# Dense expert blocks loaded in pairs of 8 KB per partition, in a hybrid decoder step on one core

## The chip, the cores and the metric

The kernel runs on one core of one Trainium2 chip. The metric is the device time of one execution in microseconds (us), taken as the median over several runs. The profile shows one profiled execution; its engines are PE (TensorE matmul), PEld (TensorE weight load), DVE (VectorE), ACT (ScalarE), POOL (GpSimd) and SP (SyncE, which issues most transfers).

## The reference, cut to what matters

One layer of a hybrid decoder for 256 prompt tokens behind 16 meta tokens and 8 running sequences of 8 tokens each. A large input projection feeds a Conformer branch and a Mamba-2 branch, and an output projection joins them. Then comes the part that the change is about, a mixer over 16384 experts (128 x 128 product keys), of which each token uses 8 heads x 16:

```python
def peer_block(xb, w_q, keys, U, V):
    q = (xb @ w_q).reshape(T, PEER_HEADS, 2, D_KEY // 2)
    s = jnp.einsum('thcd,hckd->thck', q, keys).astype(jnp.float32)
    ...
    g = jax.nn.softmax(sc, axis=-1)
    act = jax.nn.gelu(jnp.einsum('thkd,td->thk', U[ids], xb), approximate=False)
    w = (g * act).astype(xb.dtype)
    return jnp.einsum('thk,thkd->td', w, V[ids])
```

U and V hold 16384 rows of 1024 floats, 64 MB each.

## The kernel before, in words

**Weights, to 628 us.** Each projection matrix comes in blocks of 128 outputs, 512 KB, 4 KB on each of the 128 partitions. `weight` (L241) lets SP load a block into a `wraw` tile (four buffers), ACT casts it to the high part `wh` (L217), POOL subtracts it to get the low part `wl` (L218; two buffers each), and PE multiplies with both parts.

**Experts, from 628 us.** The tokens are split. For 128 tokens (and a few of the rest, `x2e`) the used rows are gathered: 144 gathers (L1080, POOL issues, queue q0), each bringing for 128 partitions one row of U and one of V, 8 KB side by side in `wuv` (five buffers). Such a *pick* is a dot product on DVE (`pick_dot`, L1192), two small ACT instructions on `scg` (gelu, then the gate, L1194 and L1195), and a weighted sum on DVE (`pick_sum`, L1200).

For the other 176 tokens every expert is computed. `u_block` (L1261) takes 128 experts of U, one of 128 blocks of 512 KB: 8 accumulating f32 matmuls on PE (L1266, two instructions each on the chip), then ACT writes the gelu of the PSUM tile into `S` (L1268). PSUM has six tiles for this, so block b + 6 waits for `S(b)`. `v_block` (L1354) multiplies the blocks of V with S in a second pass (L1357). Between them, `g_step` builds the gates of a few tokens: DVE makes one-hot matrices `oh` (L1287, L1288, L1290), PE multiplies them to `pg` (24 small matmuls, L1295), and DVE multiplies `S` by it (L1302). 22 g steps for the first half of the experts lie among u blocks 66 to 127, 22 more at the start of the second pass.

Blocks are loaded by `block` (L1254) into a ring that reuses the weights' tiles: wraw, wh, wraw, wl in turn, eight tiles of 4 KB. SP issues the loads in order and waits for each tile to be free. Between the passes SP loads `nd<-x1d` (the residual, L1324), which PE adds into the accumulators `va` (L1326). After block 122 `finish` normalises the gathered tokens, with two `wraw` tiles for its output `out_y`.

**What sets the order.** Each engine runs its instructions in the order that the Tile scheduler wrote down: DVE's picks and g steps, and ACT's `scg` and `S`, stand in one fixed row each, and an instruction that waits holds all behind it on its engine. The scheduler's own estimates of when tiles come free decide how picks and blocks interleave. Gathers are also held to the pace of the dense blocks (`gather`, L1078).

Of the kernel before, what the change touches and what calls it, by code (L numbers as in the profile page):

```python
# [7 lines left out]
F32 = mybir.dt.float32  # L8
F32R = mybir.dt.float32r
# [7 lines left out]
D = 1024  # L17
KD = 8
# [34 lines left out]
CE = 1  # L53
LOW = 400
NW0 = 3
RB = 4
OH = 2
UV = 5
GLAG = 14
# [76 lines left out]
def body(tc, ia, oa, stop=None):  # L136
    nc = tc.nc
    with ExitStack() as top:
# [10 lines left out]
        def mm(*a_, **kw):  # L149
            i_ = nc.tensor.matmul(*a_, **kw)  # L150
            if pin[0]:
                tc.keep_in_program_order(i_)
# [18 lines left out]
        o_ = VEC["conf_w"][0]  # L171
# [20 lines left out]
        def act(out, in_, f, **kw):  # L192
            i_ = nc.scalar.activation(out, in_, f, **kw)  # L193
            chain(i_)
            return i_

        def pj(name="pj"):
            return ps.tile([128, PJ], F32, name=name, tag="pj", bufs=3)[:, :T]

        def pj2(name="pj"):  # L200
            return pj(name)[:, :T2]
# [14 lines left out]
        def split(h, l, src, on_pool=False, on_dve=False):  # L216
            (nc.vector.tensor_copy if on_dve else nc.scalar.copy)(h, src)  # L217
            (nc.gpsimd if on_pool else nc.vector).tensor_tensor(l, src, h.bitcast(F32), op=OP.subtract)  # L218
# [10 lines left out]
            nc.vector.tensor_copy(dst[2 * H:2 * H + n], r_)  # L229

        S0 = NQ * TS
        rb = [RB]

        def proj(out, w, act, first=True, last=True):
            for k in range(KD):
# [2 lines left out]
            for k in range(KD):  # L238
                mm(out, w[1][:, k, :], act(k)[0], start=False, stop=(last and k == KD - 1))

        def weight(src, i):  # L241
            raw = wp.tile([128, KD, 128], F32, name="wraw", bufs=rb[0])
            nc.sync.dma_start(raw, src[i].rearrange("p (k m) -> p k m", m=128))
            h = wp.tile([128, KD, 128], F32R, name="wh", bufs=2)
            l = wp.tile([128, KD, 128], F32R, name="wl", bufs=2)
            nw[0] += 1
            f_ = lm[0]
            on_dve = int((nw[0] + 1) * f_) > int(nw[0] * f_)
            split(h, l, raw, on_pool=not on_dve, on_dve=lm[0] == 1)
            return h, l  # L250
# [6 lines left out]
        def misc(shape, name):  # L257
            return ps.tile(shape, F32, name=name, tag="misc", bufs=2)

        wp = top.enter_context(tc.tile_pool(name="wp", bufs=1))  # L260
# [8 lines left out]
        dp = dt_scope.enter_context(tc.tile_pool(name="dp", bufs=1))  # L269
# [21 lines left out]

        raws, whs, wls = [], [], []
        for i in range(3):
            r_ = wp.tile([128, KD, 128], F32, name="wraw", bufs=rb[0])
            nc.sync.dma_start(r_, ia["w_in"][(4, 5, 0)[i]].rearrange("p (k m) -> p k m", m=128))
            raws.append(r_)
            for n_, l_ in (("wh", whs), ("wl", wls)):
                l_.append(wp.tile([128, KD, 128], F32R, name=n_, bufs=2) if i < 2 else
                          dp.tile([128, KD, 128], F32R, name=n_ + "3"))
            if i == 1:  # L300
                nc.sync.dma_start(hv, ia["hv"])
        nc.sync.dma_start(vec[:, o_:], ia["vec"][:, o_:])
# [17 lines left out]
        p = misc([128, T], "pn1")  # L320
# [4 lines left out]
        on, _ = VEC["n1"]  # L325
# [7 lines left out]
        t = tp.tile([128, T], F32, name="rst", tag="yo", bufs=2)  # L333
# [504 lines left out]
        for g in range(G):  # L838
            new = ssd(g, *tiles, sz)
            if g + 1 < G:  # L840
                tiles, steps = xbc(g + 1)
# [48 lines left out]
        for j in range(KD):  # L890
# [4 lines left out]
            p = pj2()  # L895
# [7 lines left out]
        for j in range(KD):  # L903
            w = weight(ia["w_o"], j)
            p = pj2()
# [13 lines left out]
        p = ps.tile([128, T], F32, name="pn2", tag="pb", bufs=1)  # L919
        nc.tensor.matmul(p[:, :T2], ones, csum[:, :T2], start=True, stop=False)  # L920
        nc.tensor.matmul(p[:, :T2], ones, sq[:, :T2], start=False, stop=True)
        o_ = VEC["conf_w"][0]
# [33 lines left out]
        for c_ in range(2):  # L956
            p = misc([128, 512], "px")
# [4 lines left out]
        p = misc([128, 4], "prs")  # L962
# [7 lines left out]
        if NX:  # L970
# [7 lines left out]
            for c_ in range(2):  # L978
                p = misc([128, 512], "px")
# [114 lines left out]
        for j in range(16):  # L1094
            w = weight(ia["w_q"], j)
            p = pj()
# [3 lines left out]
            p = misc([128, 3, NK], "psc")  # L1100
# [149 lines left out]
                self.tasks = []  # L1250

        nraw = [0]

        def block(src, i):  # L1254
            tag, nb = (("wraw", rb[0]), ("wh", 2), ("wraw", rb[0]), ("wl", 2))[nraw[0] % 4]
            nraw[0] += 1
            raw = wp.tile([128, D], F32, name="eraw", tag=tag, bufs=nb)
            nc.sync.dma_start(raw, src[i])
            return raw.rearrange("p (k m) -> p k m", k=KD)

        def u_block(b):  # L1261
            raw = block(ia["uT"], b)
            tag, nb = (("pj", 3), ("y", 2), ("pj", 3), ("y", 2), ("pj", 3), ("pb", 1))[b % 6]
            p = ps.tile([128, PJ], F32, name="pj", tag=tag, bufs=nb)[:, :T]
            for k in range(KD):
                i_ = nc.tensor.matmul(p[:, :ND], raw[:, k, :], nd[:, k, :], start=(k == 0), stop=(k == KD - 1))  # L1266
            ustep.append(i_.ins.name)
            nc.scalar.activation(Sv(b), p[:, :ND], AF.Gelu)  # L1268
# [61 lines left out]
        def finish(tiles, load):  # L1330
            n = len(tiles)
            rs = gp.tile([128, 4, n], F32, name="frs", bufs=2)
            o = [wp.tile([128, D], F32, name="wraw", bufs=rb[0]) for _ in tiles]
            for a, (src, t0, _) in enumerate(tiles):
                nc.scalar.activation(o[a][:, :512], src[0], AF.Square, accum_out=rs[:, 0, a:a + 1])
                nc.vector.tensor_copy(o[a][:, 512:], src[1])
                nc.vector.scalar_tensor_tensor(o[a][:, 512:], o[a][:, 512:], 1.0, src[1], op0=OP.mult, op1=OP.mult,
                                               accum_out=rs[:, 1, a:a + 1])
            nc.vector.tensor_tensor(rs[:, 2], rs[:, 0], rs[:, 1], op=OP.add)
            if load:  # L1340
                tc.keep_in_program_order(nc.scalar.preload_act_table_set("natural_log_exp_and_others"))
            rstd_of(rs[:, 3], rs[:, 2], D, gp, load=False)
            for a, (src, t0, L) in enumerate(tiles):
                r_, f_ = rs[:, 3, a:a + 1], fin[0]
                for c_ in range(2):
                    cs = slice(c_ * 512, c_ * 512 + 512)
                    if a == 0 and c_ == 0:
                        nc.scalar.activation(o[a][:, cs], src[c_], AF.Copy, scale=r_)
                        nc.gpsimd.tensor_tensor(o[a][:, cs], o[a][:, cs], f_[:, cs], op=OP.mult)
                    else:  # L1350
                        nc.vector.scalar_tensor_tensor(o[a][:, cs], src[c_], r_, f_[:, cs], op0=OP.mult, op1=OP.mult)
                    (nc.sync if c_ else nc.scalar).dma_start(oa["y"][t0:t0 + L, cs], o[a][:L, cs])
# [44 lines left out]
def layout(i):  # L1397
    f = {k: np.asarray(v) for k, v in i.items()}
# [23 lines left out]
    def put(name, a):  # L1422
# [29 lines left out]
        ccache=f["cache_conf"][0].reshape(NQ, 30, 8, 128).transpose(2, 3, 0, 1).reshape(8, 128, NQ * 30),  # L1452
        state=f["state_ssm"][0].reshape(NQ, G, 256, N).transpose(1, 3, 0, 2),
        peer_uv=np.concatenate([f["peer_u"][0], f["peer_v"][0]], 1),
        uT=f["peer_u"][0].reshape(128, 128, 8, 128).transpose(0, 3, 2, 1).reshape(128, 128, D),
        vE=f["peer_v"][0].reshape(128, 128, D),
        fnorm=f["final_norm_w"],
        n2row=f["norm2_w"][0],
        fn=feat(f["final_norm_w"]),
# [31 lines left out]
```

## Time and profile before

| | us |
|---|---|
| median of 3 runs (lowest, highest) | 1382.77 (1382.6, 1384.68) |
| the profiled execution | 1380.86 |
| its span in the profile | 1379.1 |
| PE busy in it | 1317.8 |
| DVE busy | 1013.5 |
| ACT busy | 529.0 |
| POOL busy | 567.5 |

The mean clock granted to TensorE was 0.982 of full speed. In the fences of the prediction, a row of the windows gives a stretch's start and end, its length, then for each engine its busy time with the number of instructions, then the granted clock, the mean busy share of the 16 DMA engines and the GB/s that they moved. A row of the waits gives the engine, what it was about to write and its line, then what ended the wait, the time in total, how often, and the longest. A queue's row has its packets, megabytes and the time of its packets as a share of 16 engines' span. A group's row has the operation with its shapes and count, busy time, mean ns of one, and the idle time before it with what ended it. A timeline's row has start, duration, engine, line, operation, and in brackets the idle time ahead with its releaser.

### The profile page before, as it was taken

What the parts mean: (1) busy time and instruction counts of PE and PEld (TensorE: products, weight loads), DVE (VectorE), ACT (ScalarE), POOL (GpSimd) and SP (SyncE); (2) the same over time, 40 slices, a digit from 0 to 9 for tenths busy, and PEclk for the clock granted to TensorE, in tenths of its full rate; (3) what the DMA queues carried; (4) which work ended last, traced back from release to release, by engine and by line L of the source; (5) the groups of instructions that cost most, each with busy time, mean ns of one, the idle gap of its engine ahead of it and who ended that gap; (6) DMA issues with size and microseconds to landing.
All of it is one profiled execution on the core that took longest, in us unless ns stands there. A gap on an engine that the chain in (4) does not pass through costs nothing.

```text
span 1379.1 us, 24611 instructions
## 1 busy us (share of the span) xinstructions
PE 1317.8 (96%) x9328; PEld 1248.5 (91%) x9328; DVE 1013.5 (73%) x2339; ACT 529.0 (38%) x1411; POOL 567.5 (41%) x477
## 2 busy tenths in 40 slices
PE   9899999999999999998999889999969999998997
PEld 7788888888889999898998879999969999988997
DVE  7787778877877346699999867877887777775423
ACT  6687877778666445342222211112111110111001
POOL 1386776776656668452212332222232121241100
PEclk9899999999999999999999999999989999999999
DMA  6435454454343444539998999999999999999983
GB/s 236 141 120 179 161 171 136 147 165 169 126 143 120 154 152 155 172 108 351 398 413 348 393 416 413 412 367 388 399 418 415 365 393 386 400 417 414 414 307 100
DMA packets 86950, 382.05 MB, mean 277 GB/s; under 512 B 10128, under 2 KB 15632, under 8 KB 66224
## 3 DMA queue, kind: packets, MB, share of 16 engines
q1 hardware_dynamic: 64912, 227.46, 45.7%
q0 software_dynamic: 20736, 151.00, 27.0%
q10 hardware_dynamic: 1184, 2.02, 0.4%
q8 instruction: 73, 1.20, 0.4%
q14 instruction: 45, 0.37, 0.1%
HBM read 367.41 MB, written 13.03 MB: 276 GB/s over the span
## 4 chain that ended last, share of the span: by engine, by line
PE 80%; DVE 12%; DMA 5%; ACT 2%; issue 1%; POOL 0%; DVEq 0%; ACTq 0%; POOLq 0%
PE pj L150 31%; PE va L1357 21%; PE pj L1266 14%; PE pg L1295 5%; PE pst L150 2%; DMA eraw<-in_vE_dram 2%; DVE ygat L1200 2%; DMA eraw<-in_uT_dram 2%; DVE wuv L1192 2%; PE po L150 1%; PE py L150 1%; PE pdec L150 1%; DMA nd<-x1d 1%; PE ptr L155 1%; PE psc L1102 1%
## 5 line engine op out<-in xcount | busy, mean ns | idle before, releaser
L1080 POOL DMA_INDIRECT wuv<-in_peer_uv_dram,gid x144 | 175.6, 1219 | 515.9 <-DVE ygat L1200 207.4
L218 POOL TENSOR_TENSOR wl<-wraw,wh 128x1024 fp32r<-128x1024 f32 x111 | 266.9, 2406 | 177.0 <-ACT wh L217 95.6
L1266 PE MATMUL pj<-nd,eraw 128*128 128x176 f32 x2048 | 324.0, 317 | 13.3 <-DMA eraw<-in_uT_dram 8.1
L1266 PEld LDWEIGHTS pj<-nd,eraw 128*128 128x128 f32 x2048 | 310.8, 193 | 17.7 <-ACT S L1268 7.4
L1357 PE MATMUL va<-S,eraw 128*128 128x176 f32 x2048 | 314.5, 314 | 8.9 <-DMA eraw<-in_vE_dram 8.9
L1357 PEld LDWEIGHTS va<-S,eraw 128*128 128x128 f32 x2048 | 306.1, 190 | 13.0 <-DMA eraw<-in_vE_dram 11.3
L150 PE MATMUL pj<-ah,wh 128*128 128x336 f32 (+1 forms) x768 | 244.3, 329 | 2.5 <-ACT xg L193 2.2
L150 PE MATMUL pj<-al,wh 128*128 128x336 f32 (+1 forms) x768 | 234.4, 318 | 0.0
L1200 DVE SCALAR_TENSOR_TENSOR ygat<-wuv,scg,ygat 128x1024 f32<-128x1024 f32 x128 | 163.9, 1280 | 44.6 <-ACT scg L1195 41.9
L1192 DVE SCALAR_TENSOR_TENSOR wuv<-wuv,x2m 128x1024 f32<-128x1024 f32 x128 | 155.8, 1217 | 38.4 <-DMA wuv<-in_peer_uv_dram,gid 38.4
L1194 ACT ACTIVATE scg<-scg 128x1 f32<-128x1 f32 x144 | 29.0, 201 | 397.4 <-DVE wuv L1192 396.8
L217 ACT CAST wh<-wraw 128x1024 fp32r<-128x1024 f32 x125 | 131.1, 1050 | 118.1 <-PE pj L150 80.5
L471 DVE SCALAR_TENSOR_TENSOR pcv<-ccat,vec,pcv 128x256 f32<-128x256 f32 x464 | 148.5, 380 | 15.1 <-ACT pcv L469 15.1
L150 PEld LDWEIGHTS pj<-ah,wh 128*128 128x128 f32 x768 | 147.5, 192 | 10.4 <-issue 2.6
L150 PEld LDWEIGHTS pj<-al,wh 128*128 128x128 f32 x768 | 147.0, 192 | 0.7
L150 PE MATMUL pj<-ah,wl 128*128 128x336 f32 (+1 forms) x768 | 137.3, 316 | 0.0
L150 PEld LDWEIGHTS pj<-ah,wl 128*128 128x128 f32 x768 | 121.0, 189 | 0.8 <-issue 0.7
L1268 ACT ACTIVATE S<-pj 128x176 f32<-128x176 f32 x128 | 37.9, 312 | 157.7 <-PE pj L1266 157.7
L1295 PE MATMUL pg<-oh 128*128 128x64 bf16 x1056 | 75.2, 241 | 0.0
L1302 DVE TENSOR_TENSOR S<-S,pg 128x192 f32<-128x192 f32 (+1 forms) x66 | 31.7, 507 | 58.1 <-PE pg L1295 54.8
L1295 PEld LDWEIGHTS <-oh 128*128 128x128 bf16 x1056 | 71.0, 117 | 2.2
L485 DVE SCALAR_TENSOR_TENSOR pj<-mcat,vec,pj 128x360 f32<-128x360 f32 x96 | 56.4, 588 | 3.7 <-ACT pj L483 3.6
(363 smaller groups left out, 1704.6 us busy)
## 6 DMA issues: line engine op xcount, KB each, us to landing
eraw<-in_uT_dram SPq DMA_DIRECT2D x128, 512.0 KB
eraw<-in_vE_dram SPq DMA_DIRECT2D x128, 512.0 KB
wraw<-in_w_in_dram SPq DMA_DIRECT2D x80, 512.0 KB
st<-in_state_dram SPq DMA_DIRECT2D x8, 1024.0 KB
out_ssm_s_dram<-st SPq DMA_DIRECT2D x8, 1024.0 KB
wraw<-in_w_mo_dram SPq DMA_DIRECT2D x16, 512.0 KB
wraw<-in_w_q_dram SPq DMA_DIRECT2D x16, 512.0 KB
wraw<-in_w_co_dram SPq DMA_DIRECT2D x8, 512.0 KB
```

What stands on the lines that cost most here:

```text
L150: i_ = nc.tensor.matmul(*a_, **kw)
L217: (nc.vector.tensor_copy if on_dve else nc.scalar.copy)(h, src)
L218: (nc.gpsimd if on_pool else nc.vector).tensor_tensor(l, src, h.bitcast(F32), op=OP.subtract)
L471: t = nc.vector.scalar_tensor_tensor(o, i_, wv, a_, op0=OP.mult, op1=OP.add)
L485: nc.vector.scalar_tensor_tensor(o, cat[:, w:w + n], wv, o, op0=OP.mult, op1=OP.add)
L1080: i_ = nc.gpsimd.indirect_dma_start(out=u, out_offset=None, in_=ia["peer_uv"], in_offset=bass.IndirectOffsetOnAxis(ap=gid[:, c:c + 1], axi ...
L1192: nc.vector.scalar_tensor_tensor(u[:, :D], u[:, :D], 1.0, x2m if c < NPICK else x2e, op0=OP.mult, op1=OP.mult, accum_out=w)
L1200: nc.vector.scalar_tensor_tensor(a_, u[:, D:], scg[:, c:c + 1], a_, op0=OP.mult, op1=OP.add)
L1266: i_ = nc.tensor.matmul(p[:, :ND], raw[:, k, :], nd[:, k, :], start=(k == 0), stop=(k == KD - 1))
L1268: nc.scalar.activation(Sv(b), p[:, :ND], AF.Gelu)
L1295: i_ = nc.tensor.matmul(pg[:, q, :], B[:, q // 4, :, q % 4], A[:, c_, q // 4, :, q % 4], start=(c_ == 0), stop=(c_ == 2))
L1357: i_ = nc.tensor.matmul(va[k // 2][:, k % 2], raw[:, k, :], Sv(b), start=False, stop=(b == 127), skip_group_check=True)
```

## The change: pairs of blocks, and shared tiles

In DRAM the layouts `uT` and `vE` change so that two neighbouring blocks lie side by side for each partition: 64 pairs of 128 x 8 KB instead of 128 blocks of 128 x 4 KB. `block` issues one load of 1 MB for a pair and hands out its halves. The ring has four tiles of 8 KB, two with the tag `wraw` and two with `whl`, as many bytes as before. In the weights' stage two raw blocks share a `wraw` tile (`raw_half`), and the high and low part of one block share a `whl` tile (`parts`). The two output tiles of `finish` share one `wraw` tile.

```diff
-RB = 4
...
+        half = []
+
+        def raw_half():
+            if not half:
+                t = wp.tile([128, 2, KD, 128], F32, name="wraw", bufs=2)
+                half.extend((t[:, 1], t[:, 0]))
+            return half.pop()
+
+        def parts():
+            t = wp.tile([128, 2, KD, 128], F32R, name="whl", bufs=2)
+            return t[:, 0], t[:, 1]
+
         def weight(src, i):
-            raw = wp.tile([128, KD, 128], F32, name="wraw", bufs=rb[0])
+            raw = raw_half()
             nc.sync.dma_start(raw, src[i].rearrange("p (k m) -> p k m", m=128))
-            h = wp.tile([128, KD, 128], F32R, name="wh", bufs=2)
-            l = wp.tile([128, KD, 128], F32R, name="wl", bufs=2)
+            h, l = parts()
...
+        pairs = []
+
+        def ring():
+            tag = ("wraw", "whl")[nraw[0] % 2]
+            nraw[0] += 1
+            return wp.tile([128, 2 * D], F32, name="eraw", tag=tag, bufs=2)
 
         def block(src, i):
-            tag, nb = (("wraw", rb[0]), ("wh", 2), ("wraw", rb[0]), ("wl", 2))[nraw[0] % 4]
-            nraw[0] += 1
-            raw = wp.tile([128, D], F32, name="eraw", tag=tag, bufs=nb)
-            nc.sync.dma_start(raw, src[i])
-            return raw.rearrange("p (k m) -> p k m", k=KD)
+            if i % 2 == 0:
+                pairs[:] = [ring()]
+                nc.sync.dma_start(pairs[0], src[i // 2])
+            return pairs[0][:, (i % 2) * D:(i % 2 + 1) * D].rearrange("p (k m) -> p k m", k=KD)
...
-            o = [wp.tile([128, D], F32, name="wraw", bufs=rb[0]) for _ in tiles]
+            o_ = wp.tile([128, 2, D], F32, name="wraw", bufs=2)
+            o = [o_[:, a] for a in range(len(tiles))]
...
-        uT=f["peer_u"][0].reshape(128, 128, 8, 128).transpose(0, 3, 2, 1).reshape(128, 128, D),
-        vE=f["peer_v"][0].reshape(128, 128, D),
+        uT=f["peer_u"][0].reshape(64, 2, 128, 8, 128).transpose(0, 4, 1, 3, 2).reshape(64, 128, 2 * D),
+        vE=f["peer_v"][0].reshape(64, 2, 128, D).transpose(0, 2, 1, 3).reshape(64, 128, 2 * D),
```

With other tiles, the scheduler writes the engines' rows down in another order. Three places of it follow; names stand as out<-in with the shape, and in the kernel after a line has moved by 9 to 15 (L1192 is L1201, L1200 is L1209, L1268 is L1282, L1302 is L1316).

First DVE, between the `oh` of the fourth g step and that of the fifth. Before, from the end of one step to the start of the next:

```order
L1290 TENSOR_TENSOR oh<-oh,gT 128x3x256 x2
L1192 SCALAR_TENSOR_TENSOR wuv,scg<-wuv,x2m 128x1024
L1200 SCALAR_TENSOR_TENSOR ygat<-wuv,scg,ygat 128x1024
L1192 SCALAR_TENSOR_TENSOR wuv,scg<-wuv,x2m 128x1024
L1302 TENSOR_TENSOR S_7569<-S_7569,pg 128x64x8
L1287 TENSOR_TENSOR oh<-iorep,i2T 128x1024
```

Two picks' dots (L1192) stand between the two steps. The same stretch of DVE after:

```order
L1304 TENSOR_TENSOR oh<-oh,gT 128x3x256 x2
L1209 SCALAR_TENSOR_TENSOR ygat<-wuv,scg,ygat 128x1024 x2
L1201 SCALAR_TENSOR_TENSOR wuv,scg<-wuv,x2m 128x1024
L1209 SCALAR_TENSOR_TENSOR ygat<-wuv,scg,ygat 128x1024
L1201 SCALAR_TENSOR_TENSOR wuv,scg<-wuv,x2m 128x1024
L1209 SCALAR_TENSOR_TENSOR ygat<-wuv,scg,ygat 128x1024
L1201 SCALAR_TENSOR_TENSOR wuv,scg<-wuv,x2m 128x1024
L1209 SCALAR_TENSOR_TENSOR ygat<-wuv,scg,ygat 128x1024
L1201 SCALAR_TENSOR_TENSOR wuv,scg<-wuv,x2m 128x1024
L1209 SCALAR_TENSOR_TENSOR ygat<-wuv,scg,ygat 128x1024
L1316 TENSOR_TENSOR S_7378<-S_7378,pg 128x64x8
L1301 TENSOR_TENSOR oh<-iorep,i2T 128x1024
```

Now four dots stand here, and two more stand inside the step ahead of it. Counted from DVE's first pick, 40 dots stand ahead of the fifth step before and 50 after.

Second ACT, from the evacuation `S(72)` on (S_7569 before and S_7378 after are the same tile). Before, each pick is a pair of `scg` instructions between one or two evacuations:

```order
L1268 ACTIVATE S_7569<-pj 128x176
L1194 ACTIVATE scg<-scg 128x1
L1195 ACTIVATE scg<-scg,ggw 128x1
L1268 ACTIVATE S_7569<-pj 128x176 x2
L1194 ACTIVATE scg<-scg 128x1
L1195 ACTIVATE scg<-scg,ggw 128x1
L1268 ACTIVATE S_7569<-pj 128x176 x2
```

After, from `S(72)` on:

```order
L1282 ACTIVATE S_7378<-pj 128x176
L1204 ACTIVATE scg<-scg,ggw 128x1
L1203 ACTIVATE scg<-scg 128x1
L1204 ACTIVATE scg<-scg,ggw 128x1
L1203 ACTIVATE scg<-scg 128x1
L1204 ACTIVATE scg<-scg,ggw 128x1
L1282 ACTIVATE S_7378<-pj 128x176
L1203 ACTIVATE scg<-scg 128x1
L1204 ACTIVATE scg<-scg,ggw 128x1
L1282 ACTIVATE S_7378<-pj 128x176 x3
```

Counted from its first pick, ACT has 44 picks ahead of `S(78)` before and 49 after; ahead of `S(88)` 50 and 56.

Third SP, from the last loads of U to the end. Before:

```order
L1258 DMA eraw<-in_uT_dram 128x1024 x67
L1258 DMA eraw<-in_vE_dram 128x1024 x7
L1324 DMA nd<-x1d 128x1408
L1258 DMA eraw<-in_vE_dram 128x1024 x105
L952 DMA wuv<-in_fnorm_dram 128x1024
L1258 DMA eraw<-in_vE_dram 128x1024 x14
L1352 DMA out_y_dram<-wraw 128x512
L1258 DMA eraw<-in_vE_dram 128x1024
L1352 DMA out_y_dram<-wraw 16x512
L1258 DMA eraw<-in_vE_dram 128x1024
```

After:

```order
L1272 DMA eraw<-in_uT_dram 128x2048 x37
L1272 DMA eraw<-in_vE_dram 128x2048 x3
L1338 DMA nd<-x1d 128x1408
L1272 DMA eraw<-in_vE_dram 128x2048 x53
L961 DMA wuv<-in_fnorm_dram 128x1024
L1272 DMA eraw<-in_vE_dram 128x2048 x6
L1367 DMA out_y_dram<-wraw 128x512
L1272 DMA eraw<-in_vE_dram 128x2048
L1367 DMA out_y_dram<-wraw 16x512
L1272 DMA eraw<-in_vE_dram 128x2048
```

Three pairs, six blocks, stand ahead of `nd<-x1d` where seven blocks stood, and the last two pairs follow the two `out_y` where the last two blocks did.

More of the change, by code (lines that the diff above doesn't have):

```diff
@@ L231, in body @@
         S0 = NQ * TS
-        rb = [RB]
         def proj(out, w, act, first=True, last=True):
@@ L293, in body @@
         for i in range(3):
-            r_ = wp.tile([128, KD, 128], F32, name="wraw", bufs=rb[0])
+            r_ = raw_half()
             nc.sync.dma_start(r_, ia["w_in"][(4, 5, 0)[i]].rearrange("p (k m) -> p k m", m=128))
             raws.append(r_)
-            for n_, l_ in (("wh", whs), ("wl", wls)):
-                l_.append(wp.tile([128, KD, 128], F32R, name=n_, bufs=2) if i < 2 else
-                          dp.tile([128, KD, 128], F32R, name=n_ + "3"))
+            h_, l_ = parts() if i < 2 else [dp.tile([128, KD, 128], F32R, name=n_) for n_ in ("wh3", "wl3")]
+            whs.append(h_)
+            wls.append(l_)
             if i == 1:
```

## The prediction

> **What bounds the kernel now.** I read first the page's head and queues, then the windows of the last 740 us, then PE's waits there.
>
> ```profile
> span 1379.1 us, 24611 instructions
> PE 1317.8 (96%) x9328; PEld 1248.5 (91%) x9328; DVE 1013.5 (73%) x2339; ACT 529.0 (38%) x1411; POOL 567.5 (41%) x477
> q1 hardware_dynamic: 64912, 227.46, 45.7%
> q0 software_dynamic: 20736, 151.00, 27.0%
> ```
>
> PE is busy for 96%, so the whole kernel offers about 61 us of idle PE. q1 is SP's queue (weights and dense blocks), q0 the gathered rows.
>
> ```profile
> core 0: us, PE busy (x) PEld busy (x) DVE busy (x) ACT busy (x) POOL busy (x), PEclk, DMA share, GB/s
> 700.00:760.00 60.00, 56.68 (x368) 56.12 (x367) 59.72 (x204) 15.83 (x49) 13.55 (x10) 0.97 0.93 367
> 760.00:820.00 60.00, 49.93 (x331) 46.83 (x329) 46.38 (x72) 11.69 (x50) 20.71 (x14) 1.00 1.01 411
> 820.00:880.00 60.00, 59.77 (x499) 59.02 (x500) 45.27 (x71) 10.86 (x43) 14.63 (x12) 1.00 1.02 414
> 880.00:940.00 60.00, 60.00 (x508) 59.58 (x506) 45.41 (x71) 11.38 (x44) 12.64 (x11) 1.00 0.98 386
> 1000.00:1060.00 60.00, 48.85 (x394) 48.66 (x395) 48.70 (x75) 7.46 (x30) 18.69 (x16) 0.91 1.01 417
> 1180.00:1240.00 60.00, 56.65 (x402) 55.47 (x401) 42.80 (x57) 8.07 (x33) 21.22 (x16) 1.00 1.02 416
> 1240.00:1300.00 60.00, 54.45 (x357) 53.10 (x358) 30.44 (x37) 5.97 (x24) 10.18 (x9) 1.00 1.02 415
> 0.00:628.00 628.00, 612.29 (x4112) 556.76 (x4113) 456.44 (x1192) 404.56 (x951) 390.26 (x332) 0.98 0.47 154
> ```
>
> Three stages. To 628 us (weights) PE is the bound and the DMA engines are half idle. In 760 to 820 the DMA share is full and PE has holes: transfers bound it. From 820 to 1000 both are nearly full, and PE sets the pace: any time that PE loses before 880 is not won back there. In 1180 to 1300 transfers bound again.
>
> ```profile
> PE va L1326 <- DMA nd<-x1d: 11.8, 1, 11.8
> PE va L1357 <- DMA eraw<-in_vE_dram: 8.9, 8, 1.1
> PE pj L1266 <- DMA eraw<-in_uT_dram: 8.1, 8, 1.1
> PE pj L1266 <- ACT S L1268: 3.9, 3, 2.0
> ```
>
> These are PE's waits after 600 us: 28.8 us for transfers are all that faster dense loads can give.
>
> **Part 1, the packets.** Two timeline rows of the second pass and the queues at the same place:
>
> ```profile
> 1239.85 2.65 PE L1357 MATMUL va<-S,eraw 128*128 128x176 f32 x16 [1.12 <-DMA eraw<-in_vE_dram]
> 1243.60 2.65 PE L1357 MATMUL va<-S,eraw 128*128 128x176 f32 x16 [1.10 <-DMA eraw<-in_vE_dram]
> DMA packets 2001, 10.83 MB, mean 417 GB/s; under 512 B 225, under 2 KB 225, under 8 KB 1134
> q0 software_dynamic: 977, 7.09, 66.1%
> q1 hardware_dynamic: 1023, 3.72, 35.3%
> ```
>
> (The last three are of 1232 to 1258.) A block comes each 3.75 us (1243.60 less 1239.85): 0.524 MB by 3.75 is 140 GB/s, a third of 417. So beside the gathers' 8 KB packets a 4 KB packet gets every second turn and a third of the bytes. In this window 2001 less 1134, 867 packets, are of 8 KB, and q0's 66.1% of 16 x 26 us is 275 us: 317 ns each. q1 has 1134 less 225, 909 packets of 4 KB in 147 us: 162 ns each. Two old packets cost 324 ns and one new one about 317 (if SP's queue keeps 8 KB whole): the engines save 2%, no more. What changes is the share: 8 KB against 8 KB gives a dense pair half, 208 GB/s. A block is used up in 2.39 us where PE doesn't wait (9.56 us for four blocks before 999 us, shown in part 3), 219 GB/s, so the ring, eight blocks deep as before, now falls behind by 5% instead of 36%.
>
> The Trainium skill, "DMA: Bandwidth & Descriptors", section on queues and arbitration, says that each engine takes turns between queues packet by packet; the third measured here agrees. Its rules table asks for at least 1 MiB in one transfer, and its fit of 2.0 us plus bytes/436e3 would make an estimated 4.4 us for one pair alone against 6.4 for two blocks; the trace differs, since the queues run at 411 to 417 GB/s with the 512 KB loads already, so the sum takes 2%.
>
> Second pass: the 8.9 us for vE go, **-8.9** (bounds -8.9 and 0). The 8.1 for uT stand inside part 2.
>
> **Part 2, the order that comes with the other tiles.** The diff moves no line of picks, but with other tiles the scheduler puts picks earlier relative to dense blocks (the change's fences). Counted from the first row: DVE has 50 dots ahead of the `oh` of g step 4, where there were 40; ahead of steps 2 and 3 stand 44 (37 and 38), ahead of step 5 51 (42), ahead of step 9 56 (48). ACT has 49 `scg` picks ahead of `S(78)` for 44, 56 for 50 ahead of `S(88)`. PE has steps 2 and 3 ahead of block 78 and step 4 ahead of block 80. So PE reaches block 80 only when 50 rows have landed and gone through DVE. The prices:
>
> ```profile
> q1 hardware_dynamic: 7930, 28.36, 45.6%
> q0 software_dynamic: 3801, 27.73, 42.1%
> 785.86 0.20 ACT L1194 ACTIVATE scg<-scg 128x1 f32<-128x1 f32 x1 [5.83 <-DVE wuv L1192]
> 788.95 0.20 ACT L1194 ACTIVATE scg<-scg 128x1 f32<-128x1 f32 x1 [2.29 <-DVE wuv L1192]
> 791.98 0.20 ACT L1194 ACTIVATE scg<-scg 128x1 f32<-128x1 f32 x1 [2.09 <-DVE wuv L1192]
> q0 software_dynamic: 6829, 49.79, 47.2%
> 859.41 5.01 PE L1266 MATMUL pj<-nd,eraw 128*128 128x176 f32 x32
> 859.62 0.69 DVE L1302 TENSOR_TENSOR S<-S,pg 128x512 f32<-128x512 f32 x1 [0.83 <-PE pg L1295]
> 860.23 0.68 DVE L1287 TENSOR_TENSOR oh<-iorep,i2T 128x1024 bf16<-128x1024 bf16 x1
> 860.83 0.42 DVE L1288 TENSOR_TENSOR oh<-iorep,i1T 128x512 bf16<-128x512 bf16 x1
> 862.36 1.02 DVE L1290 TENSOR_TENSOR oh<-oh,gT 128x768 bf16<-128x768 bf16 x2
> L1295 PE MATMUL pg<-oh 128*128 128x64 bf16 x1056 | 75.2, 241 | 0.0
> ```
>
> The first two queue rows are of 600 to 764 us, the third of 600 to 860 (49.79 MB, 47.5 rows). By 764 there are 27.73 MB of rows (26.4 of 1.049 MB) and 28.36 of SP's, of which a last weight block is 0.5: 55.5 MB. For block 80, 50 rows are 52.4 MB; beside them the ring has landed 81 to 88 blocks, 42.5 to 46.1 MB (88 where PE is held and the ring runs full). 94.9 to 98.5 MB less 55.5, at 0.411 to 0.414 MB per us (the windows), take 95 to 105 us: 859 to 869. Behind the 50th row stand its dot, a sum or two, and the step's 0.69 + 0.68 + 0.42 + 1.02 us on DVE, then PE's 24 small matmuls (75.2 us over 44 steps, 1.7): 8 to 10 us. Block 80 starts at 867 to 879, middle 873.5. Counting blocks, before's block 80 is the row at 859.41. That is +8 to +20, middle **+14**. The second count agrees: picks back to back take 3.05 us (785.86, 788.95, 791.98), and six picks between steps 3 and 4, where there were two, are 18 us in which PE has two blocks and a step to do, about 6.3.
>
> From there PE is full (the row of 880 to 940), and the steps behind ask little more: step 9 wants 56 rows and up to 98 blocks, 110.1 MB, at 0.414 until 896, and block 90 can start behind it at 905; PE alone gets there at 873.5 + 10 x 2.39 + 5 x 1.7 = 906. The delay stays and doesn't grow. As a bound below: were the rows earlier than I take them, the term is 0, or even -8.1 (the uT waits gone); above, +20.
>
> **Clock.** After the one long wait the window of 1000 to 1060 shows a granted clock of 0.91, 0.09 x 60 = 5.4 us. If PE is now held in pieces of 5 to 10 us near block 78, the same can happen: **+1.5**, between 0 and 5.4.
>
> **Part 3, the load between the passes.** SP issues `nd<-x1d` behind three pairs instead of seven blocks.
>
> ```profile
> 989.75 9.56 PE L1266 MATMUL pj<-nd,eraw 128*128 128x176 f32 x63
> 999.35 0.33 SPq L1324 DMA_DIRECT2D nd<-x1d  x1
> 1011.15 4.44 PE L1326 MATMUL va<-nd,cst 128*128 128x176 f32 x16 [11.84 <-DMA nd<-x1d]
> ```
>
> It overwrites `nd`, so it can't leave before the last block is done (999.3) in either kernel. It is 0.72 MB; at a third to 40% of 417 GB/s that is 4.3 to 5.2 us, and the rest of the 11.8 is what stood ahead in the queue. Of three pairs, the last is issued some two blocks before the end and has had about 5 us at 208 GB/s, 1 MB. So the wait falls to 6 to 9: **-4**, between 0 and -6.
>
> **Part 4, the weights' shared tiles.** A raw tile of 8 KB comes free when both its halves have been cast and subtracted, so SP's load of a weight block waits for a neighbour more, and a pair of `wh`, `wl` comes free together.
>
> ```profile
> L217 ACT CAST wh<-wraw 128x1024 fp32r<-128x1024 f32 x125 | 131.1, 1050 | 118.1 <-PE pj L150 80.5
> L218 POOL TENSOR_TENSOR wl<-wraw,wh 128x1024 fp32r<-128x1024 f32 x111 | 266.9, 2406 | 177.0 <-ACT wh L217 95.6
> ```
>
> A block needs the cast (1.05) and then the subtraction (2.41), 3.46 us ahead of PE's matmuls on `wl`. `wh` was free once the matmuls on it were through; now the cast waits until those on `wl`, the last third of a block, are through too, some 1.2 us later (8 of 24 equal matmuls in 3.5 us). PE waits next to nothing in that stage (612 of 628 busy), and the cast's own idle time, 118 us over 125 casts, ~0.94 each, mostly after PE, says that it follows PE with slack. The later cast lies under PE's matmuls except where the slack is under 1.2. I take **+1**, between -1 and +8 (a third of 12 blocks a loss of 2).
>
> **Part 5, the tail.** The last two pairs leave SP behind the two `out_y` of the finish; pair 62 must wait for pair 60's release in any case, so it lands within a microsecond of its need: **+0.5**, 0 to +2. 64 + 64 fewer issues on SP cost and gain nothing: SP isn't waited for except for the ring.
>
> **Sum**: 14 + 1.5 - 4 - 8.9 + 1 + 0.5 = +4.1 us on the profiled execution's 1380.86 (span 1379.1 and 1.8 around): 1385. The median of three runs lies 1.9 above that execution, so against the runs the same change says 1387.
>
> **Rivals.**
> *Faster: picks do not hold PE.* If rows run ahead of the bytes I count (dense loads, with half of the bytes, no longer starve PE in 760 to 820, and the transfers' dip ahead of 760, 367 GB/s, is filled), the first pass loses nothing: 0 - 4 - 8.9 + 1.5 = -11.4, 1371; with the uT waits gone too -19.5, 1363. The 411 GB/s in 760 to 820 speak against: the bytes are the limit and 50 rows are more than the 47.5 that had landed by 860. It decides if 4 MB more, ten us of transfers, have landed by 764. Chance 0.28.
> *The change doesn't do what it says*: SP's queue still cuts packets of 4 KB. Then the 8.9 stay and the ring halves only make it coarser: +13 and upward, 1396. q0's 8 KB descriptors move whole (317 ns), which speaks against. Chance 0.08.
> *The weights' stage becomes serial.* A load issued a block later, or a cast without slack, costs 0.1 us on each of 120 blocks or 2 us on a few: +8 beyond my term, 1395. That stage's DMA share of 0.47 speaks against. Chance 0.12.
>
> **How the numbers follow.** Forecast 0.52 (its own range 1377 to 1394, from the ends of part 2 and the clock). About 0.2%, 2.8 us, can be told from no change. Below 1380 lie the first rival (0.28) and a little of the forecast's lower end (0.03): faster 0.31. Between 1380 and 1385.5 lies 0.19 of the forecast. The rest, 0.50, is slower. The range leaves out a tenth on each side: 1366 to 1397.
>
> **What would show it.** Right: the trace after has q1's packets at about half the number for the dense loads, no wait of va for vE, PE idle for some 10 us more between 840 and 880 with ACT `S` or DVE `oh` as its releaser, the last u block ending near 1014. Wrong: `pg` never waited for, and the last u block at 999 or earlier; or waits for `wh` before 628.

## The result, and the profile after

The changed kernel took 1395.89 us (median of 4 runs, 1394.56 to 1397.56) against 1382.68 (4 runs) for the kernel before: 13.2 us slower, ratio 1.0095 with a 95% interval of 1.008 to 1.011. The forecast was 1387 in a range of 1366 to 1397, with slower as the likeliest side (0.50). The profiled execution took 1397.56 us, 16.7 more than the one of before; the comparison of the two traces below explains these 16.7.

The head and the queues of the page after:

```profile
span 1395.8 us, 24215 instructions
PE 1328.3 (95%) x9328; PEld 1259.4 (90%) x9328; DVE 1018.0 (73%) x2339; ACT 522.3 (37%) x1411; POOL 573.3 (41%) x477
q1 hardware_dynamic: 46480, 227.45, 43.5%
q0 software_dynamic: 20736, 151.00, 26.9%
```

q1 moved the same bytes in 18432 packets less: 16384 of the dense loads, and 16 small ones for each of the 128 loads that are gone. So SP's queue does keep 8 KB whole. Its time fell from 45.7% to 43.5% of a slightly longer span.

The windows at the places shown of before:

```profile
core 0: us, PE busy (x) PEld busy (x) DVE busy (x) ACT busy (x) POOL busy (x), PEclk, DMA share, GB/s
700.00:760.00 60.00, 49.23 (x295) 48.15 (x294) 59.62 (x200) 14.67 (x45) 13.93 (x11) 0.91 0.90 356
760.00:820.00 60.00, 52.79 (x323) 50.73 (x322) 48.96 (x81) 12.61 (x53) 22.81 (x15) 0.95 0.95 388
820.00:880.00 60.00, 50.87 (x380) 49.34 (x378) 38.75 (x53) 9.72 (x44) 14.86 (x13) 0.96 1.01 420
880.00:940.00 60.00, 57.99 (x500) 57.68 (x501) 48.95 (x77) 11.73 (x44) 16.30 (x11) 0.95 0.95 378
1180.00:1240.00 60.00, 60.00 (x472) 59.79 (x471) 44.04 (x67) 6.96 (x28) 13.11 (x12) 1.00 1.01 411
1240.00:1300.00 60.00, 60.00 (x405) 60.00 (x404) 27.34 (x33) 5.41 (x22) 11.81 (x10) 1.00 0.99 394
```

The starvation of the second pass is gone (PE 60.00 and 60.00, where it had 56.65 and 54.45). In exchange PE has holes in 700 to 760 (49.23 for 56.68) and in 820 to 880 (50.87 for 59.77). Its waits after 600 us, with the reasons:

```profile
PE pj L1280 <- ACT S L1282: 19.1, 11, 3.9
PE va L1340 <- DMA nd<-x1d: 8.3, 1, 8.3
PE pg L1309 <- DVE oh L1304: 5.8, 1, 5.8
PE pj L1280 <- DMA eraw<-in_uT_dram: 5.6, 2, 5.1
PE va L1372 <- DMA eraw<-in_vE_dram: 2.3, 1, 2.3
```

Waits for transfers of dense blocks fell from 17.0 us to 7.9, and waits for `S` and `oh` rose from 3.9 to 24.9. PE around block 80:

```profile
854.71 2.25 PE L1280 MATMUL pj<-nd,eraw 128*128 128x176 f32 x14
860.82 4.10 PE L1280 MATMUL pj<-nd,eraw 128*128 128x176 f32 x16 [3.86 <-ACT S L1282]
865.80 2.65 PE L1280 MATMUL pj<-nd,eraw 128*128 128x176 f32 x16 [0.88 <-ACT S L1282]
868.29 3.13 PE L1309 MATMUL pg<-oh 128*128 128x64 bf16 x48
871.24 5.01 PE L1280 MATMUL pj<-nd,eraw 128*128 128x176 f32 x32
882.01 0.97 PE L1309 MATMUL pg<-oh 128*128 128x64 bf16 x13 [5.76 <-DVE oh L1304]
882.79 6.45 PE L1280 MATMUL pj<-nd,eraw 128*128 128x176 f32 x32
```

The last row is block 80, at 882.79 for 859.41. The chain of work there shows what `oh` waited for, back through DVE's row (start, length, what):

```profile
803.06 15.51 DMA wuv<-in_peer_uv_dram,gid
...
820.42 1.30 DVE ygat L1209
821.97 21.64 DMA wuv<-in_peer_uv_dram,gid
...
847.02 21.05 DMA wuv<-in_peer_uv_dram,gid
...
878.80 1.14 DVE wuv L1201 x2
882.97 6.28 PE pj L1280 x32
```

From 803 to 868 the chain is nearly all gathered rows in flight, with the DMA engines full (420 GB/s); the last 14 us ahead of block 80 are picks and a g step on DVE and ACT.

Counted by blocks (from 0) in the two traces, PE is behind by 18.8 us at block 44, by 11.6 at block 68, by 23.4 at block 80 and by 26.7 at the end of the last u block (1026.1 for 999.3). The second pass starts 23.8 late (the load between the passes costs less), is 12.6 late from block 84 on (the starvation of before, with the longer blocks behind its waits, was 11.3), and ends 16.7 late (the tail).

### The profile page after: what moved, and what is told of

Its sections match the earlier page's. It is cut to its first block, busy times and chain, and to the rows that moved or that the text cites. A ratio compares the mean times of both kernels' runs of the same rounds, so it can differ in the third digit from the quotient of the medians.

```text
span 1395.8 us, 24215 instructions
## 1 busy us (share of the span) xinstructions
PE 1328.3 (95%) x9328; PEld 1259.4 (90%) x9328; DVE 1018.0 (73%) x2339; ACT 522.3 (37%) x1411; POOL 573.3 (41%) x477
## 3 DMA queue, kind: packets, MB, share of 16 engines
q1 hardware_dynamic: 46480, 227.45, 43.5%
## 4 chain that ended last, share of the span: by engine, by line
PE 73%; DVE 15%; DMA 5%; issue 3%; ACT 2%; POOL 2%; DVEq 0%; POOLq 0%; ACTq 0%
PE pj L149 29%; PE va L1372 22%; PE pj L1280 8%; PE pg L1309 4%; DMA wuv<-in_peer_uv_dram,gid 4%; DVE ygat L1209 3%; DVE wuv L1201 2%; PE pst L149 2%; PE po L149 1%; PE py L149 1%; PE pdec L149 1%; POOL wuv L1089 1%; PE ptr L154 1%; DVE cand L1054 1%; DVE cand L1051 1%
## 5 line engine op out<-in xcount | busy, mean ns | idle before, releaser
L1089 POOL DMA_INDIRECT wuv<-in_peer_uv_dram,gid x144 | 179.2, 1245 | 521.0 <-DVE ygat L1209 141.9
L149 PE MATMUL pj<-ah,whl 128*128 128x336 f32 (+1 forms) x1520 | 372.6, 323 | 1.0 <-ACT xg L192 0.4
L1280 PE MATMUL pj<-nd,eraw 128*128 128x176 f32 x2048 | 329.8, 322 | 24.8 <-ACT S L1282 19.1
L217 POOL TENSOR_TENSOR whl<-wraw,whl 128x1024 fp32r<-128x1024 f32 x111 | 268.9, 2423 | 198.6 <-ACT whl L216 193.2
L1280 PEld LDWEIGHTS pj<-nd,eraw 128*128 128x128 f32 x2048 | 318.1, 196 | 29.7 <-ACT S L1282 23.0
L149 PEld LDWEIGHTS pj<-ah,whl 128*128 128x128 f32 x1520 | 265.5, 191 | 10.0 <-issue 3.3
L149 PE MATMUL pj<-al,whl 128*128 128x336 f32 (+1 forms) x760 | 233.5, 319 | 0.0
L1201 DVE SCALAR_TENSOR_TENSOR wuv<-wuv,x2m 128x1024 f32<-128x1024 f32 x128 | 155.9, 1218 | 71.3 <-DMA wuv<-in_peer_uv_dram,gid 71.2
L1209 DVE SCALAR_TENSOR_TENSOR ygat<-wuv,scg,ygat 128x1024 f32<-128x1024 f32 x128 | 164.0, 1282 | 46.6 <-ACT scg L1204 46.0
L216 ACT CAST whl<-wraw 128x1024 fp32r<-128x1024 f32 x125 | 130.8, 1047 | 90.6 <-PE pj L149 58.7
L149 PEld LDWEIGHTS pj<-al,whl 128*128 128x128 f32 x760 | 146.0, 193 | 0.8 <-issue 0.2
L1282 ACT ACTIVATE S<-pj 128x176 f32<-128x176 f32 x128 | 36.3, 308 | 79.5 <-PE pj L1280 79.5
L149 PE MATMUL pj<-yh,whl 128*128 128x320 f32 x256 | 56.9, 308 | 0.0
L1316 DVE TENSOR_TENSOR S<-S,pg 128x192 f32<-128x192 f32 (+1 forms) x66 | 31.5, 506 | 33.5 <-PE pg L1309 33.3
```

Of the source, the lines that this page charges most:

```text
L1089: i_ = nc.gpsimd.indirect_dma_start(out=u, out_offset=None, in_=ia["peer_uv"], in_offset=bass.IndirectOffsetOnAxis(ap=gid[:, c:c + 1], axi ...
L1201: nc.vector.scalar_tensor_tensor(u[:, :D], u[:, :D], 1.0, x2m if c < NPICK else x2e, op0=OP.mult, op1=OP.mult, accum_out=w)
L1209: nc.vector.scalar_tensor_tensor(a_, u[:, D:], scg[:, c:c + 1], a_, op0=OP.mult, op1=OP.add)
```

## The experiments

The orders of e1 to e10 are held by edges between instructions that follow each other on an engine, from the first u block on; the edges add no instruction on these engines. "Rows of before" are DVE's, ACT's and PE's in the order of the kernel before, "rows of after" in that of the changed kernel. SP's and POOL's rows are left to the scheduler but for e10. The kernel before took between 1381.6 and 1383.6 us (medians) beside these runs. No run has the changed kernel with its own rows held and nothing else, so a part of the 3 to 4 us between the change and e3, e5 or e10 may be the edges'.

**e1, pairs with the rows of before.** Edit, in the changed kernel:

```diff
         body(tc, ia, oa)
+        in_rows(tc, list(nc.cur_bb.bb.instructions))
...
+        for a, b in zip(order, order[1:]):
+            tc.add_manual_dep(seq[b], seq[a].name, NoSync)
```

> The changed kernel (pairs of 8 KB, shared tiles) with the experts' part of DVE, ACT and PE held in the row order of the kernel before; the weights' part as changed. Order theory (the time went into picks that stand earlier in ACT's and DVE's rows, so that PE waits for S and pg): the last u block ends at 990 to 1002 instead of 1026, the second pass has no vE starvation, total 1362 to 1373. Packet theory (8 KB dense packets take bandwidth from the gathered rows, for which PE then waits): the last u block still ends at 1015 or later, total 1385 to 1396. Ring theory (tiles that come free two blocks at a time make PE wait for loads): waits of pj and va for eraw of 10 us and more, total 1385 to 1396.

1374.05 us (median of 4, 1370.58 to 1379.53), ratio 0.9934 (0.9913 to 0.9955): faster than the kernel before by 8.4. The last u block ends at 999.7 although the first pass had begun 4.6 late (block 12 at 672.5 for 667.9), and the eight waits for vE of the second pass between 1230 and 1260 us are gone. In the profiled run, the slowest of the four, two others remained, at 1322 and 1356 us (e6 and e5 have their causes):

```profile
PE va L1372 <- DMA eraw<-in_vE_dram: 7.9, 2, 5.3
PE pj L1280 <- DMA eraw<-in_uT_dram: 0.2, 1, 0.2
```

The order theory's end of the first pass came, and its total was missed by 1 us (1373 at most); the other two theories are out for these rows. Where pairs and rows run side by side (1290 to 1305 us), the queues share evenly:

```profile
DMA packets 868, 6.32 MB, mean 422 GB/s; under 512 B 96, under 2 KB 96, under 8 KB 96
q0 software_dynamic: 436, 3.18, 50.8%
q1 hardware_dynamic: 432, 3.15, 50.5%
```

**e2, blocks of 4 KB with the rows of after.** Edit: the same edges with the other order, in the kernel before.

> The kernel before (blocks of 4 KB, eight tiles) with the experts' part of DVE, ACT and PE held in the row order of the changed kernel. Order theory: the last u block ends at 1020 to 1030, PE waits for ACT S some 15 to 20 us and the vE waits of 8.9 us are smaller since rows are ahead; total 1395 to 1410. Packet theory and ring theory: the last u block at 999 to 1005, total 1380 to 1388.

1384.79 us (median of 10), ratio 1.0018 (1.0008 to 1.0027). The first pass is late, as the order theory says, though by less than its numbers: block 80 at 873.1, the last u block at 1016.4, 17.0 late (1020 to 1030 expected).

```profile
PE pj L1266 <- ACT S L1268: 16.9, 10, 3.7
PE pj L1266 <- DMA eraw<-in_uT_dram: 9.9, 10, 1.2
PE va L1326 <- DMA nd<-x1d: 9.4, 1, 9.4
```

What comes last ahead of block 80 is not what it is in the change. PE waits for `uT` there, and not for `oh`:

```profile
861.75 2.63 PE L1266 MATMUL pj<-nd,eraw 128*128 128x176 f32 x16 [1.16 <-DMA eraw<-in_uT_dram]
872.02 0.96 PE L1295 MATMUL pg<-oh 128*128 128x64 bf16 x13
```

And no wait for vE is left, with 4 KB packets. The rows are ahead by then: between 1180 and 1260 us the gathers move 15.9 MB, where they moved 20.6 in the kernel before, and 11 us come back. So the total missed its range from below (1395 to 1410 expected): the order alone costs only 2.3 us.

**e3, pairs with 4 KB packets, rows of after; e4, the same with the rows of before.** Edit, in the changed kernel, with the DRAM layouts of before:

```diff
-                nc.sync.dma_start(pairs[0], src[i // 2])
+                nc.sync.dma_start(pairs[0].rearrange("p (b d) -> p b d", b=2), src[i:i + 2].rearrange("b p d -> p b d"))
```

> The changed kernel with its own rows and its tiles, but the two blocks of a pair apart in DRAM as before, so that one load of 1 MB moves 4 KB packets. Order theory: the first pass stays as in the changed kernel (last u block 1022 to 1032), and the dense loads have a third of the bytes again, so 0 to 9 us of vE starvation come back: 1394 to 1405. Packet theory: the last u block ends at 1000 to 1010, total 1378 to 1388. Ring theory: as the changed kernel, 1394 to 1400.

> The changed tiles and 1 MB loads of 4 KB packets, with the row order of the kernel before in the experts' part: against the kernel before only the tiles differ, against e1 only the packets. Order theory: as before within 5 us plus the 4 us of the tail, 1380 to 1392, with uT and vE waits of 8 to 9 us each. Packet theory: 1378 to 1388. Ring theory: 1390 to 1402, with more waits for eraw than before.

e3 took 1392.2 (ratio 1.0062, 1.0038 to 1.0085), with the last u block at 1022.3: the place that the order theory gave, the total 2 us under its range. e4 took 1393.38 (1.0079, 1.0061 to 1.0096), with the last u block at 1006.9 and, of all kernels, the most waiting for dense blocks, as the ring theory says (1390 to 1402):

```profile
PE va L1372 <- DMA eraw<-in_vE_dram: 13.1, 8, 2.4
PE pj L1280 <- DMA eraw<-in_uT_dram: 11.6, 7, 2.3
```

With e1 and e2 this makes a table (median us, and the end of the last u block in the profiled run):

| | rows of before | rows of after |
|---|---|---|
| blocks, 4 KB packets, tiles of before | 1382.5, 999.3 | 1384.8 (e2), 1016.4 |
| pairs, 4 KB packets | 1393.4 (e4), 1006.9 | 1392.2 (e3), 1022.3 |
| pairs, 8 KB packets | 1374.1 (e1), 999.7 | 1395.9 (the change), 1026.1 |

The larger packets are worth 19.3 us with the rows of before (e4 to e1) and cost 3.7 with the rows of after (e3 to the change; the two intervals, to 1.0085 and from 1.008, still touch). With the rows of before PE waits for dense blocks, and half of the bytes instead of a third feeds it. With the rows of after PE waits for gathered rows, and the dense pairs now take bytes from them: dot 48 (counted from 0) starts at 871.1 in the change, 865.7 in e3 and 855.5 in e2. So no single one of the three theories held. The new order alone costs 2.3 us, the pairs with the old order gain 8.4, and the two together cost 13.4: what the packets do has the sign that the order gives it. The coarser tiles and 1 MB loads cost 7 to 11 us with 4 KB packets (e2 to e3, before to e4); the shared output tile is in both figures, and in the 11 also a first pass that begins 4.7 us late.

**e5, the finish's output tile apart.** Edit, in the changed kernel:

```diff
-            o_ = wp.tile([128, 2, D], F32, name="wraw", bufs=2)
+            o_ = gp.tile([128, 2, D], F32, name="oy", tag="wuv", bufs=UV)
```

> The changed kernel with its own rows, but the output tile of finish taken from the gathers' buffers instead of one of the ring's two wraw tiles. Theory of the tail (the finish takes a ring tile, so pair 62 is loaded one pair ahead only, in 7 us where blocks 122 and 123 give 4.8): the wait before block 124 (2.3 us, 4.1 with the slower matmuls behind it) goes, 1390 to 1393 in total. Rival (the last pairs are late because SP issues them behind out_y): SP still has an out_y ahead of the last loads, so 2 us or more stay, 1395 to 1397.

1392.62 (ratio 1.0065, 1.0043 to 1.0088): 3.3 less than the change, in the range expected, and no wait for vE is left. In the change SP issued a pair at 1362.45 and pair 62 only at 1367.01, when pair 60 was used up; PE stood at block 124:

```profile
1374.02 11.39 PE L1372 MATMUL va<-S,eraw 128*128 128x176 f32 x64 [2.27 <-DMA eraw<-in_vE_dram]
```

SP was through with the second `out_y` at 1364.35, so it was pair 60's tile that pair 62 then waited for. With the output tile out of the ring the wait is gone, though on SP four pairs stand behind the first `out_y` there and two in the change. So the tail theory is right: the output tile took one of the ring's two `wraw` tiles.

**e7 and e8, half the gathered bytes.** These two leave out V's half of every gathered row and take U's half in its place in the weighted sum, so they don't compute the layer. Edit, in the change with its own rows (e7) and in the kernel before with its own (e8):

```diff
-            i_ = nc.gpsimd.indirect_dma_start(out=u, out_offset=None, in_=ia["peer_uv"],
+            i_ = nc.gpsimd.indirect_dma_start(out=u[:, :D], out_offset=None, in_=ia["peer_uv"],
...
-            nc.vector.scalar_tensor_tensor(a_, u[:, D:], scg[:, c:c + 1], a_, op0=OP.mult, op1=OP.add)
+            nc.vector.scalar_tensor_tensor(a_, u[:, :D], scg[:, c:c + 1], a_, op0=OP.mult, op1=OP.add)
...
-        peer_uv=np.concatenate([f["peer_u"][0], f["peer_v"][0]], 1),
+        peer_uv=f["peer_u"][0],
```

> The changed kernel with its own rows; each gather brings only the U half of a row (4 KB), and the weighted sum reads that half: half the gathered bytes, the same instructions. If PE is held near block 80 by bytes (50 rows must have landed), block 80 starts near 855 to 866 instead of 883 and the last u block ends near 1000 to 1010. If the chain dot, scg, sum, oh of each pick holds it, block 80 stays at 875 to 885. The loss between 700 and 765 us (17 us, DVE busy with the top-k) stays by either.

> The kernel before with half rows in the same way: 4 KB against 4 KB packets. The uT waits of 8.1 us and the vE waits of 8.9 go if bytes make them; block 80 at 848 to 855 instead of 859, total 1360 to 1370. It gives the floor that the old order has without a limit of transfers; against e7 the difference is the order alone.

e7 took 1370.58 us (2 runs): block 80 at 857.0 and the last u block at 999.1, where the change had 882.8 and 1026.1. The instructions and their order are the same, and after 765 us PE waits 1.3 us for `S` and never for `oh`, where the change waits 7.0 and 5.8. The hold before 765 us stayed for the most part (block 44 at 760.8, where before has 746.3 and the change 765.0). Block 80 starts here in e7 and in e8:

```profile
856.99 3.22 PE L1280 MATMUL pj<-nd,eraw 128*128 128x176 f32 x20
849.43 3.81 PE L1266 MATMUL pj<-nd,eraw 128*128 128x176 f32 x24
```

So half of the gathered bytes is worth 25.8 us at block 80 in the change and 10.0 in the kernel before. Of the 23.4 by which the change lay behind, 15.8 go with the bytes. e8 took 1355.16 (2 runs), and its total lies below the range (1360 to 1370), in part because the load between the passes cost 6.9 us instead of 11.8. With half rows the changed kernel is still 7.6 us behind at block 80 and 9.7 at the last u block; the order and the pairs' tiles are both in this.

**e10, SP's row.** In the change 23 pairs (46 blocks) stand ahead of the first transfer of the top-k's indices, `xigd`, which SP reaches early and waits at. Edit: edges on SP that put 25 pairs ahead of it, 2 more ahead of the second, as in e1.

> The changed kernel with its own rows on DVE, ACT and PE, but on SP 25 pairs (50 blocks) ahead of the first transfer of the top-k's indices (xigd) instead of 23, two more ahead of the second and three more ahead of xback, as SP's row stands in e1. In the changed kernel SP stood at xigd until 764.1 and 776.1 us with loads behind it, 44.0 blocks had landed by 764 where the blocks of e2 had 48.7, and PE waited 5.6 us for uT at block 50. If SP's row makes what the pairs cost in the first pass with these rows (e2 to e3: 5.9 us), 46 to 48 blocks have landed by 764, the wait at block 50 goes, block 80 starts at 875 to 879 instead of 883, and the total is 1389 to 1393. If the coarse release of the pairs makes it, block 80 stays at 880 or later and the total within 2 us of 1395.9.

1391.79 (4 runs, 1390.79 to 1397.6; ratio 1.0053, 1.0033 to 1.0073), but the profiled run of these is the one of 1397.6 and shows block 80 at 881.6, 1.2 earlier, and the last u block 0.4 earlier. By 764 us 27.51 MB of SP's had landed for 25.37:

```profile
q1 hardware_dynamic: 3964, 27.51, 42.4%
```

In this run the gain was given back: `xback` left at 791.8 for 781.4, the transfers fell to 316 GB/s in 760 to 790 (356 in the change), dots 34 to 40 came 3 to 8 us later, and by 800 us SP's queue was only 0.3 MB ahead. But the profiled run is the slowest. The other three took 1390.8 to 1392.1, within the 1389 to 1393 expected if SP's row makes the loss, and no trace of them was kept. So whether SP's row is what the pairs cost here stays open.

**e6 and e9, a version that beats both.** e6 is e1 with e5's tile, and `fnorm` loaded by POOL; e9 also issues by POOL the two `out_y` that SP had.

> e1 (pairs, rows of before) with the output tile of finish from the gathers' buffers and the load of fnorm issued by POOL behind the gathers instead of by SP. In e1's trace SP stood at fnorm's load until 1310 us, behind it a pair for which PE then waited 5.3 us (7.7 with the slow matmuls), and block 124 waited 2.7. If those are the cause, both go: 1362 to 1370. If the 5.3 us were the ring or the transfers (rows still landing beside 8 KB packets), they stay and only the tail goes: 1370 to 1373.

> e6 with SP's two out_y transfers issued by POOL, so that nothing but the pairs is left on SP in the second half of the last pass. In e6's trace SP stood 15.9 us at out_y until 1333.8 us with a pair behind it, for which PE waited 3.2 us (4.4 with the slow matmuls behind it). If that queueing is the cause, the wait goes and the median falls from 1371 to 1363 to 1369; if a limit of transfers made it (gathers and pairs at 210 GB/s each until 1325 us), 2 to 5 us of waits for eraw stay and the time is within 2 us of e6.

In e1 SP stood at `fnorm`, behind it seven pairs:

```profile
1310.02 0.33 SPq L961 DMA_DIRECT2D wuv<-in_fnorm_dram  x1
1310.44 33.60 SPq L1272 DMA_DIRECT2D eraw<-in_vE_dram  x7
```

In e6 that wait is gone, and `out_y` took its place until 1333.76 us: PE waited 3.2 us before block 120. e6 took 1371.22 (7 runs, 1364.55 to 1378.93; ratio 0.9912, 0.9884 to 0.9941), not clearly less than e1 and above the 1362 to 1370 expected; the median lies where the rival (a limit of transfers) put it, while the trace shows SP's queue. In e9 nothing of the second pass waits for vE:

```profile
PE va L1340 <- DMA nd<-x1d: 9.2, 1, 9.2
PE pj L1280 <- DMA eraw<-in_uT_dram: 4.2, 2, 2.5
```

1365.8 us (6 runs, 1362.42 to 1369.84), ratio 0.9875 (0.9853 to 0.9898): 15.8 us under the kernel before beside it (1381.56), the fastest here that computes everything. Its interval overlaps that of e6, so the medians don't show what moving `out_y` alone is worth.

## Why the prediction was right, and where its sizes were off

The sign, the place and the mechanism of the largest term came out; the sum of +4.1 on the profiled execution was 16.7. By the traces its parts are 26.7 for the first pass (16.5 forecast: order, clock and weights), -3.0 for the load between the passes with the slow matmuls behind it, -11.2 for the second pass and +4.1 for the tail. 1395.89 lies inside the whole range, but above the forecast's own 1377 to 1394: the room at the upper end had been made for the rivals, so that the range held is in part luck. (The ends of part 2 and of the clock, from which that own range is said to come, add up to 1379 to 1397.)

- *Packets.* 8 KB stay whole, and a pair beside gathers gets half: 3.15 MB to 3.18 in e1. The Trainium skill, "DMA: Bandwidth & Descriptors", section "Queues, rings and completion order", has the engines take turns by packets; the trace agrees with this too. The Trainium skill, "DMA: Bandwidth & Descriptors", section "Anatomy of one DMA", gives its fit of 2.0 us plus bytes/436e3 for transfers that GpSimd issues, and SP issues the dense loads; the sum did not use it. The engines save little, as forecast: 422 GB/s for 417. The -8.9 of the second pass came as -11.2, since a block behind one of the waits of before had taken 2.65 us and not 2.39. Its reason was not the only one: e2 shows the same gain by order alone.
- *Order, +14 at block 80.* The mechanism held in the change: `S` and `oh` release PE where they were forecast to, and with half the gathered bytes these waits go (e7). The size did not. With the tiles of before, block 80 starts at 873.1 (e2), the middle of the forecast to half a microsecond; but the last waits there are for `uT`, so this agreement is in part luck. The pairs add 6.3 us at block 80 by their tiles and loads (e3) and 3.4 by the packets. The mis-sized step is the bytes at hand: I took the 55.5 MB that before had moved by 764 us for the change too. By 764 the change had moved less, and e2 (third row) had not:

```profile
q0 software_dynamic: 3888, 28.31, 43.4%
q1 hardware_dynamic: 3666, 25.37, 38.8%
q1 hardware_dynamic: 7696, 27.79, 45.2%
```

That is 53.7 MB, of which about 1 is weights, against 56.1 in both the kernel before and e2. At 0.414 MB per us the 2.4 MB are 5.8 us, of the 9.3 by which block 80 missed 873.5. PE had been held before that, in 700 to 765, by picks ahead of `S` while DVE was busy with the top-k:

```profile
715.84 0.20 ACT L1203 ACTIVATE scg<-scg 128x1 f32<-128x1 f32 x1 [5.64 <-DVE wuv L1201]
716.63 21.93 PE L1280 MATMUL pj<-nd,eraw 128*128 128x176 f32 x128 [3.71 <-ACT S L1282]
```

I had read the DVE row of 700 to 760 (59.72 of 60) and ACT's order, but priced the hold at block 80 alone. This hold by itself does not make the shortfall, since e2 has it too (17.0 us at block 44, 18.8 in the change): it comes with the pairs, whose loads stopped behind SP's wait for `xigd` (e10 has 55.8 MB by 764). By 860 us the packets' share tells as well: the change has 49.0 MB of rows, e3 51.4 and e2 53.2. What the pairs add to the new order in the first pass, 5.9 us by the coarser loads and 3.8 by the packets at its end, was a term that I had with the wrong sign or not at all: by my bounds of -8.9 and 0 the packets could only help. The delay then stayed, with 3.3 us more: 23.4 at block 80, 26.7 at the end. ACT's row was miscounted: by the traces 44 and 51 picks stand ahead of `S(78)`, 49 and 57 ahead of `S(88)`, and the excerpt of the order after starts at `S(69)`; the sum went by DVE's count, which the trace confirms.
- *Clock, +1.5.* The granted clock was 0.91 in 700 to 760 and 0.95 in 880 to 940; the mean fell from 0.982 to 0.973. The 1.45 us that the 16 matmuls at 860.82 lost (4.10 for 2.65) are of the size taken, but it came at more places, and the term was too small: with the same 9328 matmuls PE's busy time rose by 10.5 us (1328.3 for 1317.8), its idle time by 6.2. Not all of the 10.5 lies on the chain, since a slow matmul ahead of another wait shortens that wait; the 32 matmuls behind the wait for `oh` (6.45 us for 5.01) do.
- *The load between the passes, -4.* The wait is 8.3 us for 11.8, -3.5.
- *Weights, +1.* The 3801st matmul of that stage starts at 604.7 for 602.4: +2.3. One wait of 1.6 us for a cast (`whl`) stands in 390 to 475 us, where before had none.
- *Tail, +0.5.* +4.1. The step that failed is "within a microsecond of its need": the load of pair 62 took 7.0 us from pair 60's release (1367.01 to 1374.02), and blocks 122 and 123 cover 4.8 of them (e5).
- *Rivals.* That picks don't hold PE is refuted by the waits for `S` and `oh`, that packets are cut by the packet count. The weights' stage lost 2.3, not 8.

Not settled: how the 5.9 us of e2 to e3 split between the release two blocks at a time, the larger loads and SP's row (e10). Also, the rows of before don't fit the changed weights' part perfectly (e1 and e4 wait 4.1 us for `sco` there), so their times may hold some us too many.

## What to carry to other kernels

Where a scheduler writes the rows, a change of tiles changes them too: hold the order by edges and measure the change and the order apart, before judging either. A larger share of the transfers for one stream helps only while that stream is the one waited for; count the bytes that must have landed for the next step, from a place where the changed kernel can be expected to have moved as many as the old one. A tile borrowed from a ring, or a transfer that waits at the head of its queue, costs the ring its lead some blocks later.

## What the runs showed of the hardware

PE's matmuls can slow down after waits that are quite short. After 0.88 to 1.17 us of idling 16 matmuls took 2.63 to 2.65 us as always; after 2.27 us, 64 took 11.39 where four blocks take 9.6; after 3.86 us, 16 took 4.10. In the kernel before, at 750.78, a wait of 1.96 us was enough (50 matmuls in 9.42 us). But the length of the wait doesn't decide alone, as e3 and e10 show, where matmuls kept their time after waits longer than 2.27 us:

```profile
1371.36 9.81 PE L1372 MATMUL va<-S,eraw 128*128 128x176 f32 x64 [3.22 <-DMA eraw<-in_vE_dram]
784.70 5.01 PE L1280 MATMUL pj<-nd,eraw 128*128 128x176 f32 x32 [2.76 <-DMA eraw<-in_uT_dram]
```

The Trainium skill, "TensorE: Matmul & The Clock Gate", Part 1, names an idle window of about 3.4 us for the slow clock; here a wait of 2.27 was enough in one place and one of 3.22 was not in another. Where the slowing came, in the waits of 2.27 and 3.86, it cost 1.4 to 1.8 us more than the wait lasted.
